# Moving the weight units to the front of SBUF, on a multiple of 512 bytes

## The chip, the cores and the metric

The kernel runs on one core of one Trainium2 chip. The time is the device time of one execution in microseconds; the median of three runs of the kernel before is 1139.0 us (1137.99 to 1139.81). All inputs lie in HBM, nearly all as float32, and the program is one launch.

## The reference, cut to what matters

One layer of a network over 256 tokens of width 1024, with 256 context tokens as a prefix:

```python
hx = modulate(x, sh1, sc1)                       # layer norm, then scale and shift from the conditioning
proj_x = hx @ w_in                               # 1024 x 2560
mix_x = concat(att_x, sgu_x) @ w_out             # neighbourhood attention and spatial gating
x = layer_norm(ALPHA * x + g1 * mix_x, ln1_g, ln1_b)
# 32 experts, the best 4 for each token, softmax over their logits
gu = t @ wgu + bgu                               # 1024 x 2048 for each expert
gate = minimum(gu[:, :1024], 7); lin = clip(gu[:, 1024:], -7, 7)
y = ((lin + 1) * (gate * sigmoid(1.702 * gate))) @ wd + bd      # 1024 x 1024 for each expert
x = layer_norm(ALPHA * x + g2 * sum(weight * y), ln2_g, ln2_b)
```

The weights of all 32 experts are read once: 12 MB for each expert, 384 MB of the 449 MB that the execution reads.

## The kernel before, in words

SBUF is used as 128 partitions. Most of it is one pool, uni, of 26 units of 8 KB per partition (NU, line 38). A unit is a tile of 128 x 2048 float32: one block of weights of 1 MB, or a work area for something else. unit() (line 105) takes the first free slot, release() gives it back.

All weights come through one list, stream. pump() (line 138) takes the next entry, gets a unit and issues its load on SP's queue; done() (line 151), called behind the last matmul on a unit, releases the unit and pumps one more. So the order of the loads is the order of use, and up to 26 units are in flight or in use. The loads are issued on lines 198 (weights of the first half), 218 (gate and up projections of the experts) and 225 (down projections). Each writes a whole unit: on each of the 128 partitions one row of 8,192 bytes. Only the last pieces of the last group are shorter (DOWN_ROWS).

The experts are done in groups of 1, 2 or 4 by rank of their load. group() runs the gate and up projections (matmuls of line 1114, one unit at a time), the activation, the down projection (line 1160) and the scatter back to the tokens. Scheduling is by the order of the program (manual_schedule); waits come from the data.

The pools are laid out in SBUF in the order in which they are opened. The first 384 bytes of each partition are taken by the program. Before the change the pool of constants cst follows from byte 384: two work tiles t2_own of 2 KB, the identity, mhalf (128 x 1, the constant -0.5), small tables, and bgu, the experts' bias. Each tile starts on a multiple of 32 bytes. cst takes 9,504 bytes, and so the first unit starts at byte 9,888, which is 32 past a multiple of 64 and 160 past a multiple of 256 and of 512; the others follow every 8,192 bytes, with the same remainder. Behind the units lie the pools mo and sm.

Places that the prediction speaks of: garow is a part of the first unit, from its element 1,632, byte 16,416 of the partition; its load has rows of 1,024 bytes (line 508). late_v["bdn"] is the part of another unit from its byte 4,096, loaded in four loads of 32 rows of 1,024 bytes (line 997). bgu is a tile of cst at byte 6,784, loaded in four loads of 32 rows of 2,048 bytes (line 862). The rows that they are read from start on a multiple of 1,024 bytes in their tensors. The temporaries of VectorE, t2(), go round in a ring: the two tiles t2_own, which start on multiples of 64, and four quarters of a unit, which start 32 past one. rsqrt() uses mhalf as an exponent:

```python
def rsqrt(var):
    r = sm.tile([P, 1], F32, tag="rs", name=nm("rs"))
    V.tensor_scalar_add(r, var, EPS)
    G.tensor_tensor(r, r, mhalf, op=ALU.pow)       # line 245
```

Of the kernel before, what the change touches and what calls it, by code (L numbers as in the profile page):

```python
# [9 lines left out]
F32 = mybir.dt.float32  # L10
# [8 lines left out]
P = 128  # L19
# [46 lines left out]
def hybrid_layer_kernel(  # L66
# [12 lines left out]
    router_w = router_w[0]  # L79
    w_gu, b_gu, w_dn, b_dn = exp_w_gu, exp_b_gu[0], exp_w_down, exp_b_down[0]  # L80

    cst = ctx.enter_context(tc.tile_pool(name="cst", bufs=1))
    uni = ctx.enter_context(tc.tile_pool(name="uni", bufs=1))
    mo = ctx.enter_context(tc.tile_pool(name="mo", bufs=2))
    sm = ctx.enter_context(tc.tile_pool(name="sm", bufs=4))
    pm = ctx.enter_context(tc.tile_pool(name="pm", bufs=4, space=bass.MemoryType.PSUM))
# [72 lines left out]
        return bass.AP(tensor=src.tensor, offset=src.offset, ap=[[0, parts], [1, n]])  # L159


    ident = cst.tile([P, P], F32, name="ident")
    make_identity(nc, ident)
    mhalf = cst.tile([P, 1], F32, name="mhalf")
    G.memset(mhalf, -0.5)


# [1249 lines left out]
```

## Time and profile before

| | us |
|---|---|
| median of three runs | 1139.0 |
| the profiled execution | 1136.04 |
| its span, first to last instruction | 1134.3 |
| TensorE matmul busy | 997.4 |
| TensorE weight load busy (beside the matmuls) | 421.6 |
| VectorE busy | 306.0 |
| ScalarE busy | 132.8 |
| GpSimd busy | 27.7 |

The mean granted TensorE clock is 0.964 of full speed. HBM is read for 449.36 MB. The page splits the span in 40 equal slices of 28.4 us; in each it gives the busy share of the engines in tenths, the busy share of the 16 DMA engines, and the rate of what they moved. A DMA packet here is one contiguous row. The time of packets is given as a share of 16 engines' time; where an engine begins a packet before the last one has ended, the share passes 100%.

### The profile page before, as it was taken

How to read it: one execution, taken by the hardware profiler on the slowest of the kernel's cores; microseconds unless marked ns; L12 is line 12 of the kernel's file. 1: busy time of each engine (PE TensorE's matmuls, PEld its weight loads, DVE VectorE, ACT ScalarE, POOL GpSimd, SP SyncE). 2: the span in 40 equal slices, each digit the busy share in tenths (PEclk: the TensorE clock that was granted, in tenths of full speed). 3: DMA queues.
4: the chain of work that ended last, by engine and by line, in shares of the span. 5: the costliest groups of instructions: out<-in, count | busy, mean ns of one | idle time of the engine just before them, and what ended most of it. 6: DMA issues, size and time to landing. Idle time of an engine off the chain costs nothing. (4 is left out here: it accounts for less than half of the span.)

```text
span 1134.3 us, 13253 instructions
## 1 busy us (share of the span) xinstructions
PE 997.4 (88%) x5140; PEld 421.6 (37%) x5140; DVE 306.0 (27%) x621; ACT 132.8 (12%) x286; POOL 27.7 (2%) x57
## 2 busy tenths in 40 slices
PE   5999897999779999986799999987799999977765
PEld 4897465333214433321253434222134343421111
DVE  6596765314103121210121212111021211201003
ACT  4343342100100101110010101000001010100000
POOL 2000300000000000000000000000000000000000
PEclk9999898999989999988999999988899999999988
DMA  9998599799999999999989999999999999999995
GB/s 381 421 396 325 229 360 366 307 386 422 420 421 421 421 420 421 422 420 421 420 343 422 421 421 420 421 422 421 421 422 420 420 422 420 421 422 421 421 420 190
DMA packets 66296, 451.32 MB, mean 398 GB/s; under 512 B 8627, under 2 KB 8883, under 8 KB 12725
## 3 DMA queue, kind: packets, MB, share of 16 engines
q1 hardware_dynamic: 66082, 450.03, 96.4%
q8 instruction: 42, 0.69, 0.2%
q10 hardware_dynamic: 148, 0.40, 0.1%
q14 instruction: 24, 0.20, 0.0%
HBM read 449.36 MB, written 1.05 MB: 397 GB/s over the span
## 5 line engine op out<-in xcount | busy, mean ns | idle before, releaser
L1114 PE MATMUL mm<-w,xg 128*32 128x512 f32 (+2 forms) x2048 | 424.9, 620 | 42.7 <-DMA w<-in_exp_w_gu_dram 42.7
L1160 PE MATMUL mm<-w,t 128*32 128x512 f32 (+2 forms) x1024 | 235.2, 645 | 52.2 <-DMA w<-in_exp_w_down_dram 43.6
L1114 PEld LDWEIGHTS mm<-w,xg 128*32 128x32 f32 (+2 forms) x2048 | 127.9, 130 | 325.6 <-issue 242.4
L1160 PEld LDWEIGHTS mm<-w,t 128*32 128x32 f32 (+2 forms) x1024 | 67.4, 133 | 207.9 <-issue 109.9
L1187 DVE TENSOR_TENSOR t<-mm,late 128x512 f32<-128x512 f32 x26 | 18.0, 692 | 263.0 <-PE mm L1160 263.0
L1130 ACT ACTIVATE t<-t 128x512 f32<-128x512 f32 x26 | 16.4, 630 | 583.0 <-DVE t L1128 583.0
L1137 DVE TENSOR_SCALAR t<-mm 128x512 f32<-128x512 f32 x26 | 18.0, 692 | 222.7 <-PE mm L1114 222.7
L1128 DVE TENSOR_SCALAR t<-mm 128x512 f32<-128x512 f32 x26 | 18.0, 691 | 215.4 <-PE mm L1114 215.4
L894 PE MATMUL mm<-bgu,sel 32*128 32x512 f32 x104 | 58.4, 641 | 4.0 <-PEq L1240 4.0
L1170 PE MATMUL ax<-t,sT 128*128 128x512 f32 x100 | 46.3, 605 | 0.8 <-DVE t L1187 0.8
L888 PE MATMUL ax<-oh,tM 128*128 128x128 f32 x384 | 44.8, 275 | 0.0
L888 PEld LDWEIGHTS ax<-oh,tM 128*128 128x128 f32 x384 | 43.8, 192 | 0.0
L1149 ACT COPY t<-ax 128x512 f32<-128x512 f32 x26 | 15.0, 576 | 190.6 <-PE ax L1145 190.6
L245 POOL TENSOR_TENSOR rs<-rs,mhalf 128x1 f32<-128x1 f32 x12 | 9.5, 797 | 1047.4 <-DVE mv L257 919.5
L1172 DVE TENSOR_TENSOR xin<-xin,ax 128x512 f32<-128x512 f32 x50 | 33.2, 684 | 5.2 <-PE ax L1170 4.8
L1170 PEld LDWEIGHTS ax<-t,sT 128*128 128x128 f32 x100 | 18.0, 189 | 29.2 <-issue 24.6
L894 PEld LDWEIGHTS mm<-bgu,sel 32*128 32x128 f32 x104 | 15.3, 183 | 34.3 <-issue 24.5
L780 ACT ACTIVATE xg<-ax,sh,sc 128x128 f32<-128x128 f32 x60 | 22.4, 457 | 32.3 <-PE ax L888 26.5
L414 DVE TENSOR_TENSOR wlo<-w,whi 128x1024 fp32r<-128x1024 f32 x20 | 23.7, 1223 | 3.1 <-ACT whi L411 3.1
L411 ACT CAST whi<-w 128x1024 fp32r<-128x1024 f32 x20 | 20.1, 1047 | 9.5 <-PE mm L446 9.5
L1145 PEld LDWEIGHTS ax<-ident,t 128*128 128x128 f32 x104 | 11.2, 141 | 21.8 <-issue 16.8
L525 DVE SCALAR_TENSOR_TENSOR accB<-w,front,accB 128x2048 f32<-128x2048 f32 x8 | 18.8, 2348 | 0.0
(261 smaller groups left out, 717.8 us busy)
## 6 DMA issues: line engine op xcount, KB each, us to landing
w<-in_exp_w_gu_dram SPq DMA_DIRECT2D x256, 1024.0 KB, 19.8
w<-in_exp_w_down_dram SPq DMA_DIRECT2D x124, 1024.0 KB, 19.8
w<-in_w_front_dram SPq DMA_DIRECT2D x38, 1024.0 KB, 10.7
w<-in_exp_w_down_dram SPq DMA_DIRECT2D x4, 512.0 KB, 16.1
w<-in_exp_w_down_dram SPq DMA_DIRECT2D x8, 256.0 KB, 6.9
T<-in_rpb_dram SPq DMA_DIRECT2D x2, 768.0 KB
xin<-in_x_dram SPq DMA_DIRECT2D x2, 512.0 KB
cin<-in_ctx_dram SPq DMA_DIRECT2D x2, 512.0 KB, 6.4
```

The lines of the kernel that those rows point to most:

```text
L411: S.copy(av[:, k], w[:, k])
L414: V.tensor_tensor(bv[:, k], w[:, k], av[:, k].bitcast(F32), op=ALU.subtract)
L525: V.scalar_tensor_tensor(accB_u, w[:, 0, :], sT[:, k, 0:1], accB_u, op0=ALU.mult, op1=ALU.add)
L780: S.activation(dst[:, kk, :], src, AF.Identity, scale=sc2[:, kk:kk + 1], bias=sh2[:, kk:kk + 1])
L888: PE.matmul(bank[:, k * P:(k + 1) * P], late["tMv"][:, t, (hh * 4 + k) * P:(hh * 4 + k + 1) * P], oh[:, t].rearrange("p n w -> p (n w)"), ...
L894: PE.matmul(b, sel[r, :], bgu[r, :], start=True, stop=False)
L1114: PE.matmul(b[a * w:(a + 1) * w, :], xg[:, half * 4 + k, a * w:(a + 1) * w], weights((gid, part, j, half, a))[:, k, :], start=False, stop= ...
L1128: V.tensor_scalar_min(gtile, b, 7.0)
L1137: V.tensor_scalar(lt, b, 7.0, -7.0, op0=ALU.min, op1=ALU.max)
L1160: PE.matmul(bank[a * w:(a + 1) * w, :], hs[kk // 4][:, kk % 4 * P + a * w:kk % 4 * P + (a + 1) * w], weights((gid, nn, r0, a))[:, k, :], s ...
L1170: PE.matmul(b, st[:, t, :], ys[nn], start=True, stop=True)
L1172: V.tensor_tensor(sl, sl, b, op=ALU.add)
```

## The change

Two lines move. A new pool, pad, is opened first, and uni second, ahead of cst; mhalf is taken from pad, as the first column of a tile of 32 float32, 128 bytes. pad then takes bytes 384 to 511, and the 26 units start at byte 512 and every 8,192 bytes after. cst, shorter by mhalf, starts behind the units, then mo and sm. The memset of mhalf stays where it was, behind the identity.

```diff
+    pad = ctx.enter_context(tc.tile_pool(name="pad", bufs=1))
+    uni = ctx.enter_context(tc.tile_pool(name="uni", bufs=1))
     cst = ctx.enter_context(tc.tile_pool(name="cst", bufs=1))
-    uni = ctx.enter_context(tc.tile_pool(name="uni", bufs=1))
     mo = ctx.enter_context(tc.tile_pool(name="mo", bufs=2))
...
+    mhalf = pad.tile([P, 32], F32, name="mhalf")[:, 0:1]
     ident = cst.tile([P, P], F32, name="ident")
     make_identity(nc, ident)
-    mhalf = cst.tile([P, 1], F32, name="mhalf")
     G.memset(mhalf, -0.5)
```

## Rows read from the trace of the kernel before

**Rows 1.** The page: span, rate in 40 slices, the queue of SP.

```profile
span 1134.3 us, 13253 instructions
...
GB/s 381 421 396 325 229 360 366 307 386 422 420 421 421 421 420 421 422 420 421 420 343 422 421 421 420 421 422 421 421 422 420 420 422 420 421 422 421 421 420 190
...
q1 hardware_dynamic: 66082, 450.03, 96.4%
```

**Rows 2.** Waits of TensorE: waiting line, releaser, total us, times, longest us.

```profile
PE mm L1160 <- DMA w<-in_exp_w_down_dram: 43.6, 35, 1.6
PE mm L1114 <- DMA w<-in_exp_w_gu_dram: 42.7, 34, 1.9
```

**Rows 3.** Stretches: busy us by engine, granted clock, DMA share, GB/s.

```profile
core 0: us, PE busy (x) PEld busy (x) DVE busy (x) ACT busy (x) POOL busy (x), PEclk, DMA share, GB/s
...
163.00:168.00 5.00, 5.00 (x54) 3.93 (x53) 3.96 (x9) 2.68 (x6) 1.28 (x1) 1.00 1.00 423
...
600.00:700.00 100.00, 99.27 (x430) 38.62 (x430) 22.22 (x44) 7.58 (x17) 0.00 (x0) 1.00 1.01 421
1000.00:1100.00 100.00, 70.02 (x335) 17.12 (x331) 8.79 (x13) 2.32 (x4) 0.00 (x0) 0.96 1.01 421
...
0.00:226.00 226.00, 201.40 (x1414) 139.87 (x1415) 143.36 (x299) 80.14 (x172) 26.52 (x55) 0.97 0.88 348
...
1119.00:1134.30 15.30, 4.25 (x11) 1.02 (x10) 8.27 (x15) 0.00 (x0) 1.22 (x2) 0.77 0.19 71
```

**Rows 4.** DMA of 226 to 1119 us; queue rows: packets, MB, share.

```profile
DMA packets 52147, 371.65 MB, mean 416 GB/s; under 512 B 5793, under 2 KB 5793, under 8 KB 7323
...
q1 hardware_dynamic: 52096, 371.01, 100.2%
```

**Rows 5.** DMA of 163 to 168 us.

```profile
DMA packets 291, 2.11 MB, mean 423 GB/s; under 512 B 33, under 2 KB 33, under 8 KB 33
...
q1 hardware_dynamic: 291, 2.11, 100.0%
```

**Rows 6.** DMA of 600 to 700 us.

```profile
DMA packets 5787, 42.11 MB, mean 421 GB/s; under 512 B 650, under 2 KB 650, under 8 KB 650
...
q1 hardware_dynamic: 5781, 42.04, 101.2%
```

**Rows 7.** DMA of 68.9 to 70.5 us, where garow's rows land.

```profile
DMA packets 231, 0.67 MB, mean 420 GB/s; under 512 B 30, under 2 KB 156, under 8 KB 191
...
q1 hardware_dynamic: 231, 0.67, 104.0%
```

**Rows 8.** DMA of 205.9 to 206.9 us, where the down bias lands.

```profile
DMA packets 222, 0.25 MB, mean 246 GB/s; under 512 B 80, under 2 KB 208, under 8 KB 208
...
q1 hardware_dynamic: 222, 0.25, 68.3%
```

**Rows 9.** DMA of 170.6 to 170.76 us, where rows of bgu land.

```profile
DMA packets 29, 0.05 MB, mean 295 GB/s; under 512 B 9, under 2 KB 9, under 8 KB 28
...
q1 hardware_dynamic: 29, 0.05, 77.6%
```

**Rows 10.** DMA issues of the three small loads: KB each, median us to landing.

```profile
bgu<-in_exp_b_gu_dram SPq DMA_DIRECT2D x4, 64.0 KB, 9.0
...
front<-in_ada_rows_dram SPq DMA_DIRECT2D x1, 128.0 KB, 8.9
late<-in_exp_b_down_dram SPq DMA_DIRECT2D x4, 32.0 KB, 3.5
```

**Rows 11.** VectorE's lines on the temporaries: shortest, median, longest ns.

```profile
L1137 DVE TENSOR_SCALAR t<-mm x26: 691/692/693, 216.5 to 1084.7; 128x512 f32<-128x512 f32 x26
...
L1128 DVE TENSOR_SCALAR t<-mm x26: 682/692/693, 208.9 to 1063.2; 128x512 f32<-128x512 f32 x26
```

**Rows 12.** Timeline of the tail: start us, length us, line, idle and releaser.

```profile
1125.22 1.22 POOL L245 TENSOR_TENSOR rs<-rs,mhalf 128x1 f32<-128x1 f32 x2 [919.52 <-DVE mv L257]
...
1130.54 0.75 DVE L1347 SCALAR_TENSOR_TENSOR xin<-xin,rs,l 128x512 f32<-128x512 f32 x1
```

## The prediction

> **What bounds the kernel now.** I read the page's head first, then the slices, then the waits, then the stretches. The span is 1134.3 us; the slice row of GB/s stands at 420 to 422 from the tenth slice on and hardly leaves it, and one queue, SP's, takes 96.4% of the time of all 16 DMA engines [rows 1]. TensorE's longest waits on anything outside itself are for the weight loads: 43.6 and 42.7 us [rows 2]. The stretches say the same more sharply: from 600 to 700 us TensorE is busy 99.27 of 100 us, from 1000 to 1100 only 70.02, and both move 421 GB/s with a DMA share of 1.01 [rows 3]. So the stream of weight units sets the time whatever the engines do, from about 226 to 1119 us. Ahead of it lies a mixed stretch (348 GB/s, DMA share 0.88), behind it a tail of 15.3 us at 71 GB/s in which VectorE, ScalarE and GpSimd finish the last rows. What the change is worth is therefore a question about one thing: how long a DMA engine holds one packet of a unit, and how often.
>
> How often: in 226 to 1119 us there are 52,147 packets, of which 7,323 are under 8 KB [rows 4]. The other 44,824 are unit rows of 8 KB, 2,800 per engine. One nanosecond per packet is thus 2.8 us of the time.
>
> How long: between 163 and 168 us the page's share of 100.0% is 16 x 5 us = 80.0 us of engine time for 258 packets of 8 KB and 33 small ones under 512 B [rows 5]. If a small one takes 9 ns, that leaves 79.7 us, 309 ns per packet. TensorE was busy 5.00 of these 5 us [rows 3]. In the long stream the packet is held longer: 600 to 700 us has 101.2% of 1600 us, 1619.2 us, for 650 small packets (5.9 us) and 5,131 large ones, 314.4 ns each [rows 6].
>
> **The change part by part.** It removes no instruction and adds none: the memset of mhalf stays behind the identity, every load keeps its queue, size and order. What moves is addresses. Units go from byte 9,888 (160 past a multiple of 256, 32 past a multiple of 64) to byte 512; the constants go behind the units; the pools mo and sm shift by 96 bytes.
>
> Does a packet's time depend on where its row starts? Three small loads of this kernel have other starts.
> - garow: 1 KB rows at byte 16,416, 32 past a multiple of 256. In 68.9 to 70.5 us, 104.0% of 25.6 us is 26.62 us for 40 packets of 8 KB (309 ns: 12.36), 30 small ones (0.27), 35 of 6 KB and 126 of 1 KB [rows 7, 10]. With the 6 KB packets on the straight line between 1 KB and 8 KB, 1 KB comes to 46.1 ns.
> - the expert bias for the down projection: 1 KB rows, 4,096 bytes into a unit, so 160 past a multiple of 256. In 205.9 to 206.9 us 68.3% of 16 us is 10.93 us, less 14 x 309 and 80 x 9 ns leaves 5.88 us for 128 packets: 45.9 ns [rows 8, 10].
> - bgu: 2 KB rows in the constants at byte 6,784, a multiple of 64 and of 128. In 170.6 to 170.76 us 77.6% of 2.56 us is 1.99 us, less one 8 KB and 9 small packets leaves 1.60 us for 19: 84.0 ns [rows 9, 10].
>
> The straight line from 1 KB (46 ns) to 8 KB (309 ns) rises by 263 ns in 7,168 bytes, 37.6 ns per KB or 1.17 ns per 32 bytes. At 2 KB it stands at 83.6 ns: the row that starts on a multiple of 64 took 84.0, no less than the units' rows would. At no length it stands at 8.4 ns, and a small packet alone takes 8 to 9 (80.0 less 79.72 us over 33 packets [rows 5], rounding included). So a unit's packet carries the fixed part that a small packet carries too, and nothing is left that I could call a price of the start, within one step of 32 bytes. I cost the new start at 0.
>
> The nearest bounds: if the whole fixed part were due to the start, 8.4 ns go; if the whole excess of the stream over the lone packet were too, another 5.4 ns (314.4 less 309). That is 13.8 x 2,800 = 38.6 us below. Above, the nearest row is the same excess once more: 5.4 x 2,800 = 15.1 us. I take 0 since the three loads with other starts are nearest to what changes, and they show none; and the excess was absent in 163 to 168 us at the same start with TensorE at 100%, so it is not the start that makes it.
>
> Here a page stands against me. The Trainium skill, DMA: Bandwidth & Descriptors, section How a descriptor splits into AXI transactions, says that a descriptor that doesn't start on a 256-byte boundary begins at the boundary below, and that the bytes ahead of its start cost time though they aren't used. By it garow's rows would be four steps of 32 bytes, 4.7 ns, cheaper than the bias rows; they took 46.1 and 45.9 ns. So the trace does not bear the rule out for the SBUF side of a load.
>
> Engine operands: the temporaries of VectorE come in turn from two tiles of the constants (multiples of 64) and four slots of a unit (32 past). L1137's 26 instructions on them last 691 to 693 ns, L1128's 682 to 693 [rows 11]. No sign of two kinds, so I cost the moved operands at 0; what hides a small error is that VectorE is busy 306 of 1134 us. In the tail nothing hides it, but the tail is 15.3 us, and 1% of that is 0.15 us. mhalf goes from byte 4,992 to 384, both multiples of 64; the last two L245 (1.22 us) stand in the tail, the last L1347 ends the compute [rows 12]. Cost 0.
>
> Sum: 0 in the stream, 0 in the mixed stretch, 0 in the tail. The profiled execution took 1136.04 us for its span of 1134.3, 0.26% under the median of 1139.0 us; the forecast is a difference of 0, put on the median: **1139.0 us**. About 0.2%, 2.3 us, is what a measurement of this kernel can tell from no change.
>
> **The rivals.**
> - One step saved. A row that starts off a multiple of 64 spills into one more step at its end than an aligned one. 1.17 ns x 2,800 = 3.3 us: 1135.7. For it: it is about the size of what my lines can't resolve, and the 8.4 ns are worked out from shares given to 0.1%. Against: 84.0 ns for bgu beside 83.6. Chance 0.13.
> - The bytes below the start are paid. At 160 past a multiple of 256 these are five steps, 5.9 ns, x 2,800 = 16.4 us: 1122.6. Against it are garow and the bias rows with equal times. For it: the packets' trace may show the read of HBM and hide a slower write behind it, which the 5.4 ns of excess in the stream leave room for. Chance 0.08. The rule of the Trainium skill's page DMA: Bandwidth & Descriptors, named above, would give this.
> - Slower: the excess grows. In the stream the 16 engines hold packets 5.4 ns longer than a lone one. If that wait is between writes and other accesses of the same SBUF rows, units that all start on a multiple of 512 could meet more often; one step more per packet is 3.3 us: 1142.3. It decides from 0.8 ns per packet on (2.3 us over 2,800). For it: the excess is there and unexplained. Against: units lie 8,192 bytes apart before and after, so their distance to each other stays, and the rate was 421 GB/s with TensorE at 70% and at 99%. Chance 0.10.
> - It doesn't do what it says: the units land elsewhere, because another small tile is put ahead of them. Then nothing happens: 1139.0. Chance 0.03, with the forecast's sign.
>
> **How the numbers follow.** No change by a packet that costs the same has 0.66. Faster by over 0.2% are the first two rivals, 0.21, and a little of the forecast's own spread: 0.22. Slower: the third, 0.10, and as little: 0.11. Within 0.2%: 0.67. The range runs from 1134, below the saved step, to 1142.5, above the longer wait; what is left out is the case at 1122.6 and the tails, under 0.2. The forecast's own range is 1136.7 to 1141.3.
>
> **What would show it.** Right: 8 KB packets still at 309 ns in a stretch like 163 to 168 us and at about 314 in the stream, 421 GB/s in every full slice, the last weight matmul at about the same time. The saved step: 308 ns and 422 to 423 GB/s. Five steps: 303 ns, or the same 309 with the excess gone, and 427 GB/s or more. Slower: 316 ns or above and 419 GB/s or less. The step that I trust least is that three loads of 1 and 2 KB, which ran outside the long stream, speak for the 8 KB packets in it. If the rate of the stream changes, it is wrong.

## The result, and the profile after

The changed kernel takes 1125.39 us (median of four runs, 1124.55 to 1126.07), the kernel before 1138.49 us beside it; the ratio is 0.9888, 95% interval 0.9867 to 0.991. That is 13.1 us less, where no change was forecast and 1134 was the low end of the range.

The page of the changed kernel, the rows that answer to [rows 1]:

```profile
span 1122.8 us, 13253 instructions
...
GB/s 384 426 398 315 246 350 375 270 389 428 425 428 426 427 427 426 426 428 426 426 356 426 427 426 427 427 426 428 426 427 426 426 427 425 428 426 428 427 425 198
...
q1 hardware_dynamic: 66082, 450.03, 96.2%
```

Same packets, same bytes, same number of instructions; but from the tenth slice on every slice of the stream moves 425 to 428 GB/s instead of 420 to 422, but for the one dip (356, before 343) and the last slice. Its stretches, with the columns of [rows 3]:

```profile
163.00:168.00 5.00, 5.00 (x66) 4.27 (x66) 4.45 (x9) 3.53 (x8) 1.52 (x1) 1.00 1.00 423
600.00:700.00 100.00, 99.27 (x439) 38.27 (x439) 21.54 (x44) 7.58 (x17) 0.00 (x0) 1.00 1.01 426
1000.00:1100.00 100.00, 72.41 (x366) 17.31 (x362) 11.46 (x17) 2.32 (x4) 0.00 (x0) 0.95 1.01 426
0.00:226.00 226.00, 201.60 (x1408) 140.59 (x1409) 143.06 (x299) 79.87 (x171) 26.54 (x55) 0.97 0.87 346
1107.00:1122.80 15.80, 4.54 (x11) 0.95 (x8) 8.28 (x15) 0.00 (x0) 1.22 (x2) 0.83 0.18 70
```

The first 226 us move 346 GB/s (348 before) and the tail lasts 15.8 us (15.3 before): no gain there. 163 to 168 us shows 423 GB/s in both. All of the gain lies in the stream: it lasted from 226 to 1119 us, 893 us, and lasts from 226 to 1107, 881 us. DMA in 163 to 168 and in 600 to 700 us, answering to [rows 5] and [rows 6]:

```profile
DMA packets 291, 2.11 MB, mean 423 GB/s; under 512 B 33, under 2 KB 33, under 8 KB 33
...
q1 hardware_dynamic: 291, 2.11, 100.0%
```

```profile
DMA packets 5853, 42.63 MB, mean 426 GB/s; under 512 B 653, under 2 KB 653, under 8 KB 653
...
q1 hardware_dynamic: 5847, 42.55, 100.8%
```

The rows of 163 to 168 us are those of before, digit for digit. In 600 to 700 us 100.8% of 1600 us, less 653 small packets at 9 ns, are 1606.9 us for 5,194 packets of SP's queue: 309.4 ns each, where it was 314.4 [rows 6]. So outside the long stream, where it took 309 ns [rows 5], the packet has not become cheaper. Its excess in the stream, 5.4 ns, is gone but for 0.4. Packets overlap a little (the shares pass 100%), so the time saved is read better from the pace, the time from one packet of an engine to its next: 1600 us over 5,194 packets is 308.0 ns for a packet and its part of the small ones, against 1600 over 5,131, 311.8 ns. 3.8 ns x 2,800 packets [rows 4] is 10.6 us; the two profiled executions differ by 1136.04 - 1124.55 = 11.5 us.

VectorE's temporaries lie at multiples of 64 on every slot now, and L1137 of before (L1139 here, two lines further down) takes what it took (691 to 693 ns):

```profile
L1139 DVE TENSOR_SCALAR t<-mm x26: 691/692/693, 217.2 to 1071.6; 128x512 f32<-128x512 f32 x26
```

### The profile page after: what moved, and what is told of

It reads as the page before. It is cut to its first block, busy times and chain, and to the rows that moved or that the text cites. A ratio compares the mean times of both kernels' runs of the same rounds, so it can differ in the third digit from the quotient of the medians.

```text
span 1122.8 us, 13253 instructions
## 1 busy us (share of the span) xinstructions
PE 986.0 (88%) x5140; PEld 421.1 (38%) x5140; DVE 306.0 (27%) x621; ACT 132.9 (12%) x286; POOL 27.8 (2%) x57
## 5 line engine op out<-in xcount | busy, mean ns | idle before, releaser
L1116 PE MATMUL mm<-w,xg 128*32 128x512 f32 (+2 forms) x2048 | 419.3, 613 | 38.8 <-DMA w<-in_exp_w_gu_dram 38.8
L1162 PE MATMUL mm<-w,t 128*32 128x512 f32 (+2 forms) x1024 | 228.9, 610 | 56.5 <-DMA w<-in_exp_w_down_dram 47.8
L1139 DVE TENSOR_SCALAR t<-mm 128x512 f32<-128x512 f32 x26 | 18.0, 692 | 217.2 <-PE mm L1116 217.2
L896 PEld LDWEIGHTS mm<-bgu,sel 32*128 32x128 f32 x104 | 15.3, 183 | 34.0 <-issue 24.2
```

Source lines behind the costliest of these rows:

```text
L896: PE.matmul(b, sel[r, :], bgu[r, :], start=True, stop=False)
L1116: PE.matmul(b[a * w:(a + 1) * w, :], xg[:, half * 4 + k, a * w:(a + 1) * w], weights((gid, part, j, half, a))[:, k, :], start=False, stop= ...
L1139: V.tensor_scalar(lt, b, 7.0, -7.0, op0=ALU.min, op1=ALU.max)
L1162: PE.matmul(bank[a * w:(a + 1) * w, :], hs[kk // 4][:, kk % 4 * P + a * w:kk % 4 * P + (a + 1) * w], weights((gid, nn, r0, a))[:, k, :], s ...
```

## The experiments

Twelve kernels were run, in three sets. The first set was meant to show that a multiple of 64 is what counts. The first edit below is against the kernel before, all others are against the changed kernel. Ratios are to the kernel before, run beside each.

**32 bytes ahead of the constants of the kernel before.** Units at 9,920.

```diff
+    fill = cst.tile([P, 8], F32, name="fill")
     ctx.enter_context(tc.manual_schedule())
```

> The kernel before with 32 bytes put ahead of its constants: all places move by 32 bytes, the order of the pools stays. The units start at byte 9,920, a multiple of 64, 192 past a multiple of 256. Theory A (rows off a multiple of 64 make the 8 KB packets wait in the full stream): the wait goes, 306 ns from packet to packet, 426 GB/s, 1125 us, ratio to before 0.989. Theory B (bytes below the start, down to a multiple of 256, are paid): six steps of 32 bytes instead of five, so slower than before, about 1141 us, ratio 1.002; the change would then have won its 13 us by going from five steps to none. Theory C (what counts is that the constants and small pools moved behind the units): as before, 1138 us, ratio 1.0. Theory D (a multiple of 512 is needed): as before, 1138 us.

Measured: 1137.96 us, ratio 0.9996 (0.9981 to 1.0012). Theory A fell as I had put it: a multiple of 64 brings nothing. B's growing price fell too: six steps cost no more than five.

**The changed kernel with the pad cut to 32 bytes.** Units at 416.

```diff
-    mhalf = pad.tile([P, 32], F32, name="mhalf")[:, 0:1]
+    mhalf = pad.tile([P, 8], F32, name="mhalf")[:, 0:1]
```

> The changed kernel with a pad of 32 bytes instead of 128: units first and constants behind as changed, but the units start at byte 416, 32 past a multiple of 64 and 160 past a multiple of 256, the remainders of before. A: all of the gain is lost, 1138 us, 421 GB/s, ratio to before 1.0. B: 1138 us too (five steps). C: the gain stays, 1125 us, ratio 0.989. D: 1138 us.

Measured: 1137.94 us, ratio 0.9998 (0.9982 to 1.0014). The order of the pools is that of the changed kernel, and the whole gain is lost. So it is not the new place of the constants (theory C), it is where the units start.

**The changed kernel with a pad of 64 bytes.** Units at 448 (`[P, 16]` in the same line).

> The changed kernel with a pad of 64 bytes: units at byte 448, a multiple of 64 but not of 128, 192 past a multiple of 256. A: as the changed kernel, 1125 us, 426 GB/s, ratio 0.989. B: six steps, 1141 us, ratio 1.002. C: 1125 us. D, or a need for a multiple of 128: 1138 us.

Measured: 1138.21 us, ratio 1.0 (0.9981 to 1.002). A and C missed; a multiple of 64 is not enough in this layout either. B missed too (1141). Of the theories only D, or a need for some multiple above 64, had all three of these times right.

**Half of the units 32 bytes off a multiple of 64.**

```diff
-    uni = ctx.enter_context(tc.tile_pool(name="uni", bufs=1))
+    uni_a = ctx.enter_context(tc.tile_pool(name="uni_a", bufs=1))
+    gap = ctx.enter_context(tc.tile_pool(name="gap", bufs=1))
+    uni_b = ctx.enter_context(tc.tile_pool(name="uni_b", bufs=1))
+    gap.tile([P, 8], F32, name="gap_t")
...
-        t = uni.tile([P, 2048], dt, tag=f"u{i}", name=nm(name))
+        t = (uni_b if i % 2 else uni_a).tile([P, 2048], dt, tag=f"u{i}", name=nm(name))
...
-    mhalf = pad.tile([P, 32], F32, name="mhalf")[:, 0:1]
+    mhalf = pad.tile([P, 16], F32, name="mhalf")[:, 0:1]
```

> The changed kernel with its units in two pools of 13: even ones from byte 448 (multiples of 64), odd ones 32 bytes further, 32 past a multiple of 64; 194 of 431 unit loads in the program go to odd ones. A, with a price that each packet off the multiple pays for itself: 45% of the 13 us is lost, 1131 us, ratio 0.994, 424 GB/s. A, with a wait that needs two packets off the multiple to meet: 0.45 squared, about 20% lost, 1128 us. A, with a wait that any packet off the multiple brings to all engines: above 1133 us. B: 1142 us. C: 1125 us.

Measured: 1142.1 us, ratio 1.0032 (1.0014 to 1.0051). It says little of shares, since with starts at 192 and 224 past a multiple of 256 no unit was in a good place, as the next set showed. The time is B's, but B had missed two of the three runs beside it, those at 9,920 and at 448 (1141 expected, 1138 measured).

The second set asked which multiple it is: 128, 256 or 512.

**Units at 384:** mhalf back among the constants, nothing ahead of the units.

```diff
-    mhalf = pad.tile([P, 32], F32, name="mhalf")[:, 0:1]
+    mhalf = cst.tile([P, 1], F32, name="mhalf")
```

> The changed kernel without a pad (mhalf back among the constants): units at byte 384, a multiple of 128, 128 past a multiple of 256. The runs before this one have put a multiple of 64 out of the question (1138 us at 9,920 and at 448). Theory A128 (a multiple of 128 is enough): 1125 us, ratio to before 0.989. Theory A256 (a multiple of 256 is needed, and any other start costs the same): 1138 us, 421 GB/s, 310 ns from packet to packet. Theory D (a multiple of 512): 1138 us.

Measured: 1138.65 us, ratio 0.9994 (0.9979 to 1.0008). A multiple of 128 is not enough.

**Units at 768:** the edit of the last one, and two tables ahead of the units.

```diff
-    tri = cst.tile([P, P], BF16, name="tri")
+    tri = pad.tile([P, P], BF16, name="tri")
...
-    keyb = cst.tile([P, NE], F32, name="keyb")
+    keyb = pad.tile([P, NE], F32, name="keyb")
```

> The changed kernel with two tables of the constants (tri and keyb, 384 bytes) in the pool ahead of the units: units at byte 768, a multiple of 256 but not of 512. A128 and A256: 1125 us, 426 GB/s, 306 ns from packet to packet, ratio 0.989. D: 1138 us, ratio 1.0.

Measured: 1124.93 us, ratio 0.9885 (0.9869 to 0.9902). A multiple of 256 is enough; 512 is not needed.

**Units at 544,** 32 past a multiple of 512: keyb and a mhalf of 32 bytes ahead of them.

```diff
-    mhalf = pad.tile([P, 32], F32, name="mhalf")[:, 0:1]
+    mhalf = pad.tile([P, 8], F32, name="mhalf")[:, 0:1]
...
-    keyb = cst.tile([P, NE], F32, name="keyb")
+    keyb = pad.tile([P, NE], F32, name="keyb")
```

> The changed kernel with keyb (128 bytes) and a mhalf of 32 bytes ahead of the units: units at byte 544, 32 past a multiple of 256 and of 512. A256 with one price for any start off the multiple: 1138 us, ratio 1.0, 421 GB/s. A price that grows with the distance from the multiple below (one step of 32 bytes here, five in the kernel before): about 1128 us, ratio 0.991.

Measured: 1141.17 us, ratio 1.0025 (1.0015 to 1.0034). The smallest distance was no cheaper than 128, 160 or 192; it was the dearest of the four. One price for any start off the multiple (1138) is not quite right either: the interval of the ratio lies above 1. DMA in 600 to 700 us, first of the kernel at 768, then of the one at 544:

```profile
DMA packets 5857, 42.67 MB, mean 427 GB/s; under 512 B 652, under 2 KB 652, under 8 KB 652
...
q1 hardware_dynamic: 5851, 42.59, 100.9%
```

```profile
DMA packets 5761, 42.00 MB, mean 420 GB/s; under 512 B 637, under 2 KB 637, under 8 KB 637
...
q1 hardware_dynamic: 5756, 41.94, 101.0%
```

5,199 packets against 5,119 in the same 100 us: 307.8 and 312.6 ns of pace.

**Half of the units at multiples of 512, half 32 bytes past:** the two pools of the fourth experiment, with keyb ahead of the first and mhalf (32 bytes) between them.

> The changed kernel with its even units from byte 512 (multiples of 512) and its odd ones 32 bytes past such a multiple; 194 of 431 unit loads go to odd ones. A price that each packet off the multiple pays for itself: 45% of the loss, 1131 us, ratio 0.994, 424 GB/s, with 308 ns from packet to packet on average. A wait that only two packets off the multiple give each other: 1128 us. A wait that one such packet brings to all engines: 1135 us or more.

Measured: 1131.51 us, ratio 0.9943 (0.9927 to 0.996), just where a price that each packet pays for itself would put it. The profile does not bear that out. Three stretches of the kernel at 768, then of this one, and the last of them for the kernel with all units at 544 (columns as in [rows 3]):

```profile
0.00:226.00 226.00, 202.30 (x1406) 140.55 (x1407) 142.79 (x299) 80.01 (x171) 26.58 (x55) 0.96 0.86 345
560.00:605.00 45.00, 44.27 (x130) 21.02 (x129) 8.45 (x18) 4.09 (x9) 0.00 (x0) 0.98 0.92 384
605.00:1100.00 495.00, 436.33 (x2077) 150.15 (x2079) 82.96 (x156) 26.87 (x58) 0.00 (x0) 0.97 1.01 426
```

```profile
0.00:226.00 226.00, 201.11 (x1397) 140.31 (x1399) 142.76 (x298) 79.91 (x171) 26.52 (x55) 0.96 0.86 341
560.00:605.00 45.00, 44.27 (x129) 21.00 (x128) 8.12 (x18) 4.08 (x9) 0.00 (x0) 0.96 0.90 371
605.00:1100.00 495.00, 435.83 (x2057) 152.44 (x2056) 80.57 (x153) 26.83 (x58) 0.00 (x0) 0.97 1.01 425
```

```profile
605.00:1100.00 495.00, 437.11 (x2034) 151.35 (x2032) 80.31 (x152) 26.86 (x58) 0.00 (x0) 0.97 1.01 419
```

In the long stretch from 605 us on the half-off kernel runs at 425 GB/s, 1 below the good one, where the kernel with all units off moves 419: about a seventh of the way and not 45%. It isn't that this stretch uses few odd units: by the order in which the kernel hands out its units, the odd ones take 7 to 11 of every 20 loads from the first to the last. Its further loss lies ahead of 226 us (4 GB/s less over 226 us, 0.9 MB, some 2 us) and around the pause of the stream at 560 to 605 us (13 GB/s over 45 us, 0.6 MB, 1.4 us). So the time fits one theory, the pace the other, and the runs do not settle how a packet off the multiple beside one on it is charged.

The third set asked whose wait it is: the DMA's own, or a meeting with the engines that read the units.

**The stream alone.** All loads of the experts (384 blocks of 1,048,576 bytes, 402.7 of the 449.4 MB that the kernel reads) and nothing else, at 416 and at 512 bytes. The code is cut, and PADW and PIECES stand here for the numbers beside them:

```python
pad_t = pad.tile([P, PADW], F32, name="pad_t")      # 8 (byte 416) or 32 (byte 512)
...
def load(src):
    t = uni.tile([P, 2048], F32, tag=f"u{n[0] % 24}", name=f"w_{n[0]}")
    n[0] += 1
    for h in range(PIECES):                          # 1, or 2 for rows of 4 KB
        w = 2048 // PIECES
        SP.dma_start(t[:, h * w:(h + 1) * w], src[:, h * w:(h + 1) * w])
for e in range(NE):
    for i in range(8):
        load(exp_w_gu[e][i])
    for i in range(4):
        load(exp_w_down[e][i])
...                                                  # zeros into a tile, and from it to the output
```

> The stream by itself: the 384 expert blocks of 1 MB are loaded one after the other on SP's queue into 24 units in a ring, and no engine reads them; all computing is left out and zeros are written. Units at byte 416, 160 past a multiple of 256 as in the kernel before. 3,072 packets of 8 KB per engine. Theory W (the wait is the DMA's own): 310 ns from packet to packet as in the kernel before, 421 GB/s, about 954 us of stream plus some us at the ends. Theory X (the wait comes from meeting TensorE's and the other engines' accesses of the units): 306 ns, 426 to 427 GB/s, about 942 us, the same as at byte 512.

> The same stream by itself with the units at byte 512. W: 306 ns from packet to packet, 942 us, 12 us (1.3%) less than at byte 416. X: 942 us, the same as at byte 416.

Measured: 964.4 us at 416 (964.27 and 964.53), 951.74 us at 512 (951.72 and 951.77). 12.7 us over 3,072 packets is 4.1 ns for each. No engine touches the units here, so the wait is the DMA's own: W, not X. DMA of the stream alone at 416 in 600 to 700 us:

```profile
DMA packets 5792, 42.20 MB, mean 422 GB/s; under 512 B 641, under 2 KB 641, under 8 KB 641
...
q1 hardware_dynamic: 5792, 42.20, 101.4%
```

The same at 512:

```profile
DMA packets 5871, 42.73 MB, mean 427 GB/s; under 512 B 655, under 2 KB 655, under 8 KB 655
...
q1 hardware_dynamic: 5871, 42.73, 101.1%
```

By the working of the prediction the packet takes 313.8 ns at 416 and 309.0 ns at 512: the excess over 309 ns is there at 416 and gone at 512. And three stretches at 416, near its start, a little later and in the middle (busy VectorE and GpSimd, clock, DMA share, GB/s), then the first two at 512:

```profile
8.00:16.00 8.00, 0.00 (x0) 0.00 (x0) 1.00 1.01 426
32.00:40.00 8.00, 0.00 (x0) 0.00 (x0) 1.00 1.01 421
600.00:700.00 100.00, 0.00 (x0) 0.00 (x0) 1.00 1.01 422
```

```profile
8.00:16.00 8.00, 0.00 (x0) 0.00 (x0) 1.00 1.01 427
32.00:40.00 8.00, 0.00 (x0) 0.00 (x0) 1.00 1.02 429
```

Near its start the stream off the multiple runs at 426 GB/s, within 1 of the stream on it. The wait is not there yet; from 32 us on it is. The stretch of 163 to 168 us of the kernel before looks alike: it too follows a time in which the queue was not full (231 GB/s from 140 to 145 us).

**Rows of 4 KB,** twice as many packets for the same bytes.

> The stream by itself at byte 416 with each block loaded in two halves, rows of 4 KB: 6,144 packets per engine. By the 8 KB packet's 306 ns and the slope of 1.17 ns per 32 bytes a 4 KB packet takes about 156 ns when it doesn't wait, 959 us in all. A price per packet (4 ns each, twice as many): 24 us more than at byte 512. A price per byte (2 ns for each): 12 us more.

> The stream by itself at byte 512 with rows of 4 KB: 156 ns from packet to packet, about 959 us, under either price, since no row starts off a multiple of 256 (the second half starts 4,096 bytes later).

Measured: 995.93 us at 416, 971.91 us at 512. The difference is 24.0 us, 3.9 ns for each of 6,144 packets: a price per packet, not per byte. At 512 the stream took 13 us more than my 959; some 10 of these stand at the ends, as for rows of 8 KB (951.74 against 942). DMA in 600 to 700 us at 416, then at 512:

```profile
DMA packets 11247, 40.96 MB, mean 410 GB/s; under 512 B 1248, under 2 KB 1248, under 8 KB 11247
```

```profile
DMA packets 11537, 42.01 MB, mean 420 GB/s; under 512 B 1281, under 2 KB 1281, under 8 KB 11537
```

1600 us over 9,999 and 10,256 packets of 4 KB are 160.0 and 156.0 ns. Here too the price comes late: from 8 to 16 us both streams move 397 GB/s, from 16 to 24 us the one at 416 moves 410 and the one at 512 moves 417.

No run pointed to a kernel faster than the changed one: 768 (1124.93) and 512 (1125.39) agree within their spread.

## Why the prediction was wrong

**What bounds the kernel** was right: the stream of weights at one rate, 2,800 packets per engine, 2.8 us for each nanosecond. The price per packet was wrong, and with it the sum.

**The step that failed** is the choice of 0 for the new start, against the excess of the stream: "the excess was absent in 163 to 168 us at the same start with TensorE at 100%, so it is not the start that makes it." All but 0.4 of the 5.4 ns of excess went when the start moved. It comes up only once the stream has run for a while. The stream alone at 416 shows the same with no engine at work: 426 GB/s from 8 to 16 us, 421 and 422 later. A stretch without the wait showed that a bad start need not cost anything at once; I read it as showing that it never does.

**The three small loads proved nothing.** I set garow (32 past a multiple of 256), the bias rows (160 past) and bgu (128 past) beside each other and found the same time for the same length [rows 7 to 9]. All three lie off a multiple of 256, and the experiments put the boundary there: 544, 416, 448 and 384 give 1141, 1138, 1138 and 1139 us; 512 and 768 give 1125. So I compared bad starts with bad starts. But a good start would have shown me no more. In the changed kernel the bias rows start on a multiple of 256; DMA of the changed kernel in 207 to 208 us, where 98 of them land:

```profile
DMA packets 160, 0.10 MB, mean 101 GB/s; under 512 B 62, under 2 KB 160, under 8 KB 160
...
q1 hardware_dynamic: 160, 0.10, 31.7%
```

31.7% of 16 us is 5.07 us; less 62 small packets at 9 ns, 4.51 us are left for 98 rows, 46.1 ns each. They took 45.9 ns at 160 past [rows 8]. These loads run outside the long stream, which I had named as the step I trusted least, and there neither they nor the packets of 8 KB show a price at either start.

**The fixed part.** The 309 ns of 163 to 168 us stand after as before (291 packets, 100.0%). So that half of the working held: nothing was to be had from the 8.4 ns. (That a small packet takes 8 to 9 ns was not a check of it: the 309 ns had been got by giving a small packet 9.) The bound that I worked out for the excess, 5.4 x 2,800 = 15.1 us, was the right term, and I set it to 0. By pace it measured 3.8 ns, 10.6 us, against 11.5 between the profiled executions and 13.1 between medians.

**The rivals.** One step saved (1135.7) and the longer wait (1142.3) did not come. The second, at 1122.6 with a chance of 0.08, was nearest, and one of its signs came: the same 309 ns with the excess gone, at 426 GB/s. But its sum was five steps of 32 bytes below the start, and a price that grows with these steps fell at 544 and at 9,920, so that it came near is in part luck. The slower write behind the read, which I gave as a reason for it, no run shows. The rule of the Trainium skill, DMA: Bandwidth & Descriptors, section How a descriptor splits into AXI transactions, has two halves for what is fetched: a boundary of 256 bytes, and a cost for the bytes from the boundary to the start. For loads into SBUF the runs bear out the boundary (1125 us at 768 and 512, 1138 and more off it) and not the cost by distance (1141 us at 32 past, 1138 at 160 and 192). I had let garow speak against both halves, and its rows show no price at all.

**Engine operands** at 0 was right as far as the runs go: at 416 constants and units had the order of the changed kernel, at 384 VectorE's temporaries lay on multiples of 64 in every slot as well, and both times were that of before. The stream alone shows a difference of 12.7 us with no engine at work.

**What stays open.** The runs show when the wait is there, not what waits for what. A packet off the multiple costs about 4 ns on average, at 8 KB as at 4 KB, only in a stream that has run some time; half of the units off the multiple cost far less than half of the pace in the long stretch. Two accounts are argued and not shown. One is a write side slightly slower than the read side, with slack that a stream first uses up. The other is a price for blocks of 256 bytes: a row of 8 KB that starts off a multiple of 256 touches 33 of them and not 32, one of 4 KB 17 and not 16, one more in both and at any distance. It would fit a price per row that does not grow with the distance, and the two could hold together. Neither was tried by itself, and neither says why 32 past is dearer than 160. Starts at 64, 96 and 224 past a multiple of 256 were not run by themselves.

## What to carry to other kernels

Where a kernel is bound by loads into SBUF, put the tiles that receive them on a multiple of 256 bytes of the partition; here it gave 1.1% for no work. Take a packet's price from the stretch that binds, at full load, not from small loads elsewhere or from the first microseconds after a pause. Before a trace is used to rule a cost out, make sure that it holds both cases under the load that binds; if all its samples lie on one side, or away from that load, the question is still open, and the whole unexplained excess belongs into the range.

## What the runs showed that I had not expected

- The step is at a multiple of 256 bytes: 128 past a multiple of 256 (byte 384, 1138.65 us) is as bad as 160 past, 256 past a multiple of 512 (byte 768, 1124.93 us) is as good as 0.
- 32 past is a little worse than the other bad starts: 1141.17 us, ratio 1.0025 (1.0015 to 1.0034) to the kernel before.
- The price is per row: 4.1 ns for rows of 8 KB, 3.9 ns for rows of 4 KB, and it is not there in the first microseconds of a stream.
- Rows of 4 KB instead of 8 KB cost more than the start does: 971.91 against 951.74 us for the same 384 blocks at byte 512.
